# Differential attention beside a gated linear recurrence: no activation-table changes in the attention, the rotation on VectorE, both score maps as row tiles, and a three-part pool

## The chip, the cores and the metric

One Trainium2 chip, one core of it. The metric is the device time of one execution in microseconds (us). The kernel is written in Bass with its tile framework: the order on TensorE (PE) is the program's own, the other engines (VectorE, DVE; ScalarE, ACT; GpSimd, POOL; SyncE, SP) get their order from a scheduler that goes by priorities and dependencies. Line numbers L.. are those of the kernel before, unless the text says otherwise.

## The reference

One layer on 512 latent tokens (T) with 256 context tokens (C) ahead of them, width 1024. Three branches read the same modulated input: A, a bidirectional RG-LRU behind a convolution of width 4; B, differential attention with rotary positions, 8 heads of two maps with 64 dimensions each; C, a gated MLP. Cut to what the change touches:

```python
def diff_attn_core(q, k, v, lam):
    s = jnp.einsum('bqhmd,bkhmd->bhmqk', q.astype(f32), k.astype(f32)) * (DIFF_HEAD_DIM ** -0.5)
    p = jax.nn.softmax(s, axis=-1)
    w = p[:, :, 0] - lam * p[:, :, 1]
    return jnp.einsum('bhqk,bkhe->bqhe', w, v.astype(f32)).astype(v.dtype)
...
def diff_head_out(o, g, lam_init):
    of = o.astype(f32)
    of = of * lax.rsqrt(jnp.mean(jnp.square(of), axis=-1, keepdims=True) + RMS_EPS)
    of = of * g.astype(f32) * (1.0 - lam_init)
```

Each branch is multiplied by a SiLU gate (z * sigmoid(z)) of its own projection, projected, merged by sigmoid gates, projected again, and added to the input under a layer norm.

## The kernel before

Everything is float32 in and out. A product of two float32 matrices is made of three products of parts: each operand is split into a high part in the engine's rounded float32 (fp32r) and a low part, the rest, and TensorE adds high x high, high x low and low x high (`mm3`, L62 to L64; `proj_cm` for a whole projection of 24 products). Splitting is a cast on ScalarE and a subtraction (`split`, L54 and L55). Weights come by DMA on SP's queue in the order of a list of wants (`want`, L193 on), in pieces of 128 x 1024, and are split in `w_conv` (L121 the cast, L122 the subtraction, on POOL during the attention and on VectorE behind it).

The work goes in stages. A head (0 to 60 us) makes the modulated input. A prologue (60 to 98) projects q, k and v of the first heads. The attention (98 to 396) has 32 steps, one for each head h and block qt of 128 queries: `scores` (L705) makes both maps' scores, 768 keys each, into two of three PSUM buffers of 1024 columns; `softmax` takes the maximum (L715, VectorE) and the exponential (L720, ScalarE) of each and scales the first by 1/sum (L723); `combine` subtracts the second times lambda (L728 to L730, VectorE). Between the scores and the transposes of the step before (`transp`, L735, whose result is split in `wt_split`, L746 and L748) the hand-written plan puts units of projections for later heads: k, context k (kc), q, v, and the gate gb. Their evacuation is cut into chores that are handed out between units: `z_evac` (L512, ScalarE), `rope` (a shuffle L521, z times the cosine on POOL L522, the shuffled times the sine L524, the sum L525), then the split of q (`q_evac`, L542, L547) and k (`k_split`, L565, L570).

For the scores the high and low part of a map stand on the two halves of the 128 partitions of k: map 0 has its high part on partitions 0 to 63 and its low part on 64 to 127, map 1 the other way round. One product with K=128 then does two of the three at once, and needs q's parts on both halves, which a DMA on POOL's queue copies (L549). So a step has 8 products, four of 512 and four of 256 columns.

When a head's four blocks are done, `values` multiplies with v, squares on ScalarE (L755), evacuates (L756, VectorE), and `rms` sums the squares with a product with ones, takes Ln (L762) and Exp (L763) and multiplies on POOL (L764). The gate of the head takes a sigmoid (L670). Exponential, Ln and sigmoid are in different activation tables, and each change is an ACT_TABLE_LOAD on ScalarE.

The recurrence's stage (396 to 644) begins with the last transposes, the first block's projection xa0, head 7's values and its rms, the context's projection xac0; `conv_in` (L865, L867) evacuates both into `pad`, `conv` and `conv_split` make the input of the gate products ri. For each of 8 blocks follow the projections, the gates, the scans, the block's SiLU gate (`branch_a`, ga, which writes the block's result to DRAM in pa_d, L947), and the merge of branch B (`merge_gate` gt1, `merge_b` y1, which reads hsB, the split of all heads' outputs ob).

Behind it (from 644) pa_d is loaded back into pa on SP's queue (L1026) and split into hsA (L54, L55), and branch C begins: `proj_tokens` projects 16 pieces sv, each added on VectorE to the bias bvv (L1041 into vz), a load on SP's queue behind those of pa (L1031).

Of the kernel before, what the change touches and what calls it, by code (L numbers as in the profile page):

```python
# [22 lines left out]
H = 8  # L23
# [6 lines left out]
def block_kernel(ctx, tc, x, c, cctx_in, c_ctx, w_ada, b_ada, w_in, b_in, conv_w, conv_b,  # L30
# [193 lines left out]
    V.memset(tiny, 2.0 ** -100)  # L224
    sc16 = cp.tile([P, 16], F32, name="sc16")
# [18 lines left out]
    with tc.tile_pool(name="hd", bufs=1) as hd:  # L244
# [186 lines left out]
        S.preload_act_table_set("natural_log_exp_and_others")  # L431
# [72 lines left out]
    def z_evac(ps, b, name):  # L504
# [6 lines left out]
        z = at.tile([P, T], F32, tag="z", bufs=2, name="z" + name)  # L511
# [16 lines left out]
    def q_evac(h, ps):  # L528
# [5 lines left out]
        def hi():  # L534
            qds[h] = at.tile([P, 4, T], F32R, tag="qd", bufs=2, name="qd" + n)
            qd = qds[h]
            for m in range(2):
                a = slice(64 * m, 64 * m + 64)
                if h < 2:
                    S.mul(qd[a, 2 * m, :], z[a], 0.125)  # L540
                else:
                    V.tensor_scalar(qd[a, 2 * m, :], z[a], 0.125, None, op0=ALU.mult)  # L542

        def fin(m):
            qd = qds[h]
            a, b = slice(64 * m, 64 * m + 64), slice(64 - 64 * m, 128 - 64 * m)
            V.scalar_tensor_tensor(qd[a, 2 * m + 1, :], z[a], 0.125, f(qd[a, 2 * m, :]),  # L547
                                   op0=ALU.mult, op1=ALU.subtract)
            G.dma_start(qd[b, 2 * m:2 * m + 2, :], qd[a, 2 * m:2 * m + 2, :])  # L549
        chore(0.7, n, hi, 4 * h - 5)  # L550
        chore(0.6, n, lambda: fin(0))
        chore(0.6, n, lambda: fin(1))

    def k_split(n, h, z, sl):

        def hi():
            if h not in kds:
                kds[h] = at.tile([P, 2, TA], F32R, tag="kd", bufs=2, name=f"kd{h}")
            kd = kds[h]
            for m in range(2):  # L560
                a = slice(64 * m, 64 * m + 64)
                if n[1:] in "01":
                    S.copy(kd[a, m, sl], z[a])
                else:
                    V.tensor_copy(kd[a, m, sl], z[a])  # L565

        def lo(m):
            kd = kds[h]
            a, b = slice(64 * m, 64 * m + 64), slice(64 - 64 * m, 128 - 64 * m)
            V.tensor_tensor(kd[b, m, sl], z[a], f(kd[a, m, sl]), ALU.subtract)  # L570
        w = (sl.stop - sl.start) / 960
        chore(w + 0.15, n, hi, 4 * h - 5)
        chore(w + 0.07, n, lambda: lo(0))
        chore(w + 0.07, n, lambda: lo(1))
# [47 lines left out]
    def units(kind, i):  # L622
# [39 lines left out]
        def u():  # L662
# [7 lines left out]
            S.activation(sg, ps, AF.Sigmoid, bias=bcol(40 + i))  # L670
# [608 lines left out]
```

## Time and profile before

| | us |
|---|---|
| median of 3 runs | 1037.99 |
| lowest and highest run | 1035.18, 1039.12 |
| the profiled execution's own time | 1038.81 |
| its span in the trace | 1037.0 |
| TensorE (PE) busy | 974.0 (94%) |
| VectorE (DVE) busy | 663.6 (64%) |
| ScalarE (ACT) busy | 526.1 (51%) |
| GpSimd (POOL) busy | 155.7 (15%) |

The span is that of the profiled instructions; the execution's own time has 1.8 us around it. Busy time of TensorE counts a product to its modelled end, so the start times of products tell more than their lengths. A share of the whole span is an average over stages with different limits, so the rows below are those of single stages, waits and stretches. The granted clock (PEclk) is 1.00 at full speed.

### The profile page before, as it was taken

The numbers are of one execution on the slowest core, as the hardware profiler recorded it, in microseconds if no ns is written. First come the engines' busy times: TensorE is split into PE (matmuls) and PEld (weight loads), VectorE is DVE, ScalarE is ACT, GpSimd is POOL, SyncE is SP. The second block draws the span as 40 slices with busy tenths as digits, with TensorE's granted clock in tenths as the row PEclk, the third lists the DMA queues.
The fourth block names the chain that finished last, engine by engine and source line by source line (L and its number), as shares of the span: only waits on it lengthen the run. The fifth ranks groups of instructions, "written<-read, shape, count | busy, mean of one in ns | idle before, by whom it ended". The sixth has DMA issues, their size and how long they took to land.

```text
span 1037.0 us, 14225 instructions
## 1 busy us (share of the span) xinstructions
PE 974.0 (94%) x5719; PEld 844.0 (81%) x5719; DVE 663.6 (64%) x1024; ACT 526.1 (51%) x741; POOL 155.7 (15%) x117
## 2 busy tenths in 40 slices
PE   5997799989989998999999999599999999999996
PEld 4796688878878886888888888598889988888896
DVE  4479788788788663787777776348433356424567
ACT  3145856647647796897777794213231234332221
POOL 2143424333243252000000000000000000000002
PEclk8999999989989999999999999799999999999998
DMA  9933220130130132113333223534332232654312
GB/s 299 296 103 84 62 61 21 42 101 21 41 102 21 41 102 70 43 51 102 102 102 92 82 92 92 189 107 132 95 99 82 82 102 82 236 171 145 98 61 82
DMA packets 148184, 103.41 MB, mean 100 GB/s; under 512 B 3629, under 2 KB 143382, under 8 KB 148118
## 3 DMA queue, kind: packets, MB, share of 16 engines
q1 hardware_dynamic: 146054, 96.11, 30.4%
q0 software_dynamic: 1920, 6.29, 2.3%
q8 instruction: 45, 0.74, 0.3%
q14 instruction: 21, 0.17, 0.1%
q10 hardware_dynamic: 144, 0.10, 0.0%
HBM read 94.10 MB, written 4.19 MB: 95 GB/s over the span
## 4 chain that ended last, share of the span: by engine, by line
PE 66%; DVE 16%; ACT 10%; DMA 4%; issue 3%; SPq 1%; POOL 0%; POOLq 0%; ACTq 0%; DVEq 0%
PE y L62 4%; PE gt L62 4%; PE gt L64 4%; PE gt L63 4%; PE y L64 4%; PE y L63 4%; DVE mxn L715 2%; DVE e L730 2%; DVE kd L565 2%; PE out L62 1%; PE u L62 1%; PE u L64 1%; PE u L63 1%; PE out L64 1%; PE out L63 1%
## 5 line engine op out<-in xcount | busy, mean ns | idle before, releaser
L121 ACT CAST w<-raw 128x1024 fp32r<-128x1024 f32 x96 | 99.7, 1044 | 83.5 <-PE y L64 20.0
L122 DVE TENSOR_TENSOR w<-raw,w 128x1024 fp32r<-128x1024 f32 x71 | 86.4, 1222 | 66.9 <-ACT w L121 66.9
L62 PE MATMUL gt<-xhl,w 128*128 128x512 f32 x192 | 75.6, 394 | 1.3 <-ACT pad L865 1.3
L63 PE MATMUL gt<-xhl,w 128*128 128x512 f32 x192 | 74.8, 390 | 0.0
L64 PE MATMUL gt<-xhl,w 128*128 128x512 f32 x192 | 74.8, 390 | 0.0
L705 PE MATMUL s<-kd,qdq 128*128 128x512 f32 (+1 forms) x256 | 58.7, 368 | 15.6 <-ACT e L720 6.0
L122 POOL TENSOR_TENSOR w<-raw,w 128x1024 fp32r<-128x1024 f32 x25 | 61.0, 2445 | 67.4 <-ACT w L121 67.4
L705 PEld LDWEIGHTS s<-kd,qdq 128*128 128x128 f32 x256 | 44.5, 196 | 27.1 <-issue 12.7
L715 DVE TENSOR_REDUCE mxn<-s 128x1 f32<-128x768 f32 x64 | 58.3, 949 | 7.5 <-PE s L705 7.5
L720 ACT ACTIVATE e<-s,mxn 128x768 f32<-128x768 f32 x32 | 28.8, 900 | 50.9 <-DVE mxn L715 50.8
L1162 POOL PARTITION_BROADCAST grb<-grs x8 | 3.8, 581 | 322.4 <-DVE grs L1159 322.4
L62 PEld LDWEIGHTS gt<-xhl,w 128*128 128x128 f32 x192 | 36.1, 188 | 9.1 <-ACT pad L865 1.5
L64 PEld LDWEIGHTS gt<-xhl,w 128*128 128x128 f32 x192 | 36.0, 188 | 7.7
L63 PEld LDWEIGHTS gt<-xhl,w 128*128 128x128 f32 x192 | 36.1, 188 | 7.0
L947 POOL DMA_DIRECT2D pa_d<-ha x8 | 4.4, 551 | 227.4 <-DVE ha L946 227.4
L730 DVE SCALAR_TENSOR_TENSOR e<-s,sm,e 128x768 f32<-128x768 f32 x32 | 32.6, 1017 | 6.5 <-ACT e L723 5.7
L54 ACT CAST vh<-v 128x128 fp32r<-128x128 f32 x48 | 12.4, 264 | 42.7 <-PE v L64 19.5
L842 ACT ACT_TABLE_LOAD x25 | 32.1, 1283 | 0.5
L62 PE MATMUL xa<-xhl,w 128*128 128x512 f32 x64 | 26.3, 411 | 4.8 <-ACT pad L865 4.8
L748 DVE TENSOR_TENSOR wtl<-t,wth 128x768 fp32r<-128x768 f32 x32 | 30.3, 950 | 0.6 <-ACT wth L746 0.5
L723 ACT ACTIVATE e<-e,sm 128x768 f32<-128x768 f32 x32 | 29.9, 934 | 0.2 <-DVE sm L722 0.2
L842 ACT ACTIVATE rt<-ri,colB 128x770 f32<-128x770 f32 x32 | 27.7, 906 | 2.5 <-PE ri L64 1.8
(457 smaller groups left out, 3233.0 us busy)
## 6 DMA issues: line engine op xcount, KB each, us to landing
raw<-in_w_in_dram SPq DMA_DIRECT2D x96, 512.0 KB, 3.9
raw<-in_w_branch_dram SPq DMA_DIRECT2D x24, 512.0 KB, 4.0
ada<-in_w_ada_dram SPq DMA_DIRECT2D x6, 1024.0 KB, 9.6
qdq<-qdq POOLq DMA_DIRECT2D x16, 256.0 KB, 3.2
adg<-in_w_ada_dram SPq DMA_DIRECT2D x8, 512.0 KB, 6.6
raw<-in_w_out_dram SPq DMA_DIRECT2D x8, 512.0 KB, 3.4
xtok<-in_x_dram SPq DMA_DIRECT2D x4, 512.0 KB, 5.7
ada<-in_w_ada_dram SPq DMA_DIRECT2D x4, 512.0 KB, 5.9
```

The lines of the kernel that those rows point to most:

```text
L62: PE.matmul(ps, ah, bh, start=(first and i == 0), stop=False)
L63: PE.matmul(ps, ah, bl, start=False, stop=False)
L64: PE.matmul(ps, al, bh, start=False, stop=(last and i == n - 1))
L121: S.copy(h, raws[j])
L122: state["lo"].tensor_tensor(l, raws[j], f(h), ALU.subtract)
L705: PE.matmul(sp[:, sl], qds[h][:, 2 * m + j, qs], kds[h][:, m, sl], start=(j == 0), stop=(j == 1))
L715: V.tensor_reduce(mxn[:, m:m + 1], sps[m][:, 0:TA], mybir.AxisListType.X, ALU.max, negate=True)
L720: S.activation(e, sps[m][:, 0:TA], AF.Exp, bias=mxn[:, m:m + 1], accum_out=sm[:, m:m + 1])
L723: S.mul(es[i][0], es[i][0], sm[:, 0:1])
L730: V.scalar_tensor_tensor(e0, e1, sm[:, 1:2], e0, op0=ALU.mult, op1=ALU.add)
L748: V.tensor_tensor(wts[h][1][:, :, qs], src, f(wts[h][0][:, :, qs]), ALU.subtract)
L842: order[0] = S.activation(out, in_, fn, **kw)
```

## The change

It has five parts.

- **No table changes in the attention.** The gate's sigmoid(x) becomes 0.5 * tanh(0.5 x) + 0.5 in two ScalarE passes, tanh being in the exponential's table. `rms` keeps only the mean square: the product with 32 columns of ones writes 32 rows, which are copied into msb, four heads one above the other. Ln and Exp are taken once for all heads behind head 7. The 8 rows of 1/rms go to DRAM by 8 DMAs on POOL's queue, come back on SP's queue to all partitions (rsb, in five loads on two shared buffers), and `hs_b` multiplies them into ob on VectorE and splits ob into hsB.
- **Rotation on VectorE alone.** The product with the cosine moves from POOL to VectorE.
- **Both maps side by side.** q and k keep map 0 on partitions 0 to 63 and map 1 on 64 to 127, with the high and the low part in two planes; high parts are made on ScalarE in one instruction for both maps, low parts on VectorE in one. The copying DMAs go. Each of the three products has K=64 and a tile position of its own, row 0 or row 64, and the two maps alternate: 12 products a step.
- **Softmax and evacuation.** The second map's exponential goes to SBUF in place of PSUM. The evacuation of o moves from VectorE to ScalarE.
- **The pool in three parts.** mp (msb, sq), a1 (the rotation's tiles, z, zc) and at (the rest). a1 is released at step 28 and its space taken by l1, into which the recurrence's first weights are loaded there. In TensorE's order xac0 comes ahead of head 7's values, xa1, xac1 and a gate gt1 ahead of the first gates ri. Behind the recurrence bvv is loaded ahead of pa, and the last piece of pa by POOL's queue.

```diff
@@ rope @@
-            G.tensor_tensor(z, z, ropc, ALU.mult)
-        chore(0.6, name, c0)
+            V.tensor_tensor(z, z, ropc, ALU.mult)
+        chore(1.3, name, c0)
@@ q_evac @@
+            qds[h] = at.tile([P, 2, T], F32R, tag="qd", bufs=2, name="qd" + n)
+            S.mul(qds[h][:, 0, :], z, 0.125)
+
+        def lo():
             qd = qds[h]
...
-            G.dma_start(qd[b, 2 * m:2 * m + 2, :], qd[a, 2 * m:2 * m + 2, :])
+            V.scalar_tensor_tensor(qd[:, 1, :], z, 0.125, f(qd[:, 0, :]),
                                    op0=ALU.mult, op1=ALU.subtract)
@@ k_split @@
+            S.copy(kds[h][:, 0, sl], z)
...
+            V.tensor_tensor(kd[:, 1, sl], z, f(kd[:, 0, sl]), ALU.subtract)
@@ the gate gb, in units @@
-            S.activation(sg, ps, AF.Sigmoid, bias=bcol(40 + i))
+            S.activation(sg, ps, AF.Tanh, bias=hb[:, i:i + 1], scale=0.5)
+            S.activation(sg, sg, AF.Identity, bias=halfc, scale=0.5)
...
-            S.preload_act_table_set("natural_log_exp_and_others")
@@ scores @@
+        sps = [big_t(f"s{i}_{m}") for m in range(2)]
+        for sl in (slice(0, 512), slice(512, TA)):
+            for j, (jq, jk) in enumerate(((0, 0), (0, 1), (1, 0))):
+                for m in range(2):
+                    a = slice(64 * m, 64 * m + 64)
+                    PE.matmul(sps[m][:, sl], qds[h][a, jq, qs], kds[h][a, jk, sl],
+                              start=(j == 0), stop=(j == 2), tile_position=(64 * m, 0))
@@ softmax @@
-            e = sps[1][:, 0:TA]
-            if m == 0:
-                e = at.tile([P, TA], F32, tag="e0", bufs=2, name=f"e0_{i}")
+            e = at.tile([P, TA], F32, tag=f"e{m}", bufs=2 - m, name=f"e{m}_{i}")
@@ values @@
-        V.tensor_scalar(ob[:, h, :], ps, vbias[:, h:h + 1], gcol, op0=ALU.add, op1=ALU.mult)
+        S.activation(ob[:, h, :], ps, AF.Identity, bias=vbg[:, h:h + 1], scale=gcol)
@@ rms @@
-        PE.matmul(pm, ones, sq, start=True, stop=True)
-        S.activation(sq, pm, AF.Ln, bias=epst)
-        S.activation(sq, sq, AF.Exp, scale=-0.5)
-        G.tensor_tensor(ob[:, h, :], ob[:, h, :], sq, ALU.mult)
+        r = slice(32 * (h % 4), 32 * (h % 4) + 32)
+        PE.matmul(pm[r, 0:T], ones[:, 0:32], sq, start=True, stop=True,
+                  tile_position=(0, 32 * (h % 4)))
+        order[0] = S.copy(msb[r, h // 4, :], pm[r, 0:T])
@@ in the loop over steps @@
+        if i == 28:
+            a1.release()
+            l1 = tc.alloc_tile_pool(name="l1", bufs=1, side="right", reuse_waits="tile")
+            lru_dma(0)
+            pad = pad_alloc()
@@ behind the loop @@
+    with tc.high_priority():
+        conv_in(0, ps, True)
+    ps = acc_t("xac0")
+    proj_cm(ps[:, 0:TC], W, C, 0, TC)
+    with tc.high_priority():
+        conv_in(0, ps[:, 0:TC], False)
+        conv(0)
+        lru_hi(0)
     sqs.append((7, values(7, big_t)))
...
+    act(msb, msb, AF.Ln, bias=epst)
+    act(msb, msb, AF.Exp, scale=-0.5)
+    for h in range(H):
+        r = 32 * (h % 4)
+        G.dma_start(rs_d[h:h + 1, :], msb[r:r + 1, h // 4, :])
...
+    def hs_b(n, hs_):
+
+        rsb = mp.tile([P, len(hs_), T], F32, tag=("sq", "msb")[len(hs_) - 1], name=f"rsb{n}")
+        for j, h in enumerate(hs_):
+            nc.sync.dma_start(rsb[:, j, :], rs_d[h].partition_broadcast(P))
+        for j, h in enumerate(hs_):
+            V.tensor_tensor(ob[:, h, :], ob[:, h, :], rsb[:, j, :], ALU.mult)
+            split(hs[:, 0, h, :], hs[:, 1, h, :], ob[:, h, :])
@@ in the recurrence's loop @@
+        if i == 0:
+            merge_gate(0)
...
+        if i == 0:
+            for n, hs_ in enumerate(((0, 1), (2,), (3, 4), (5,), (6, 7))):
+                hs_b(n, hs_)
@@ behind it @@
-    for g in range(8):
-        nc.sync.dma_start(pa[:, g, :], pa_d[g])
+    for g in range(7):
+        nc.sync.dma_start(pa[:, g, :], pa_d[g])
+    G.dma_start(pa[:, 7, :], pa_d[7])
```

How the built programs' orders differ at three places. A name's numbers tell its buffers apart; rows read line, operation, out<-in, shape. First TensorE, the third step's scores behind the transposes (t) of the step before. Before:

```order
L735 MATMUL t_1178<-ident,e_2_1075 128x128 x6
L705 MATMUL s_0_1192<-kd_737,qdq_778 128x512 x2
L705 MATMUL s_0_1192<-kd_737,qdq_778 128x256 x2
L705 MATMUL s_1_1197<-kd_737,qdq_778 128x512 x2
L705 MATMUL s_1_1197<-kd_737,qdq_778 128x256 x2
L62 MATMUL q_1214<-xhl,w_995 128x512
```

and with the change:

```order
L727 MATMUL t_1193<-ident,e_2_1085 128x128 x6
L700 MATMUL s_0_1204<-kd_776,qdq_780 128x512
L700 MATMUL s_1_1205<-kd_776,qdq_780 128x512
L700 MATMUL s_0_1204<-kd_776,qdq_780 128x512
L700 MATMUL s_1_1205<-kd_776,qdq_780 128x512
L700 MATMUL s_0_1204<-kd_776,qdq_780 128x512
L700 MATMUL s_1_1205<-kd_776,qdq_780 128x512
L700 MATMUL s_0_1204<-kd_776,qdq_780 128x256
L700 MATMUL s_1_1205<-kd_776,qdq_780 128x256
```

Six pairs (the last four products of 256 columns are left out) take the place of eight products, and neither map is done before the other.

Next ScalarE where head 6's rms and a gate fall, in steps 26 and 27: sq is the squares, ms their sum, lw the recurrence's weights, sgb the gate, e the exponentials. Before:

```order
L762 ACT_TABLE_LOAD
L762 ACTIVATE sq_3196<-ms_3241,epst 128x512
L763 ACT_TABLE_LOAD
L763 ACTIVATE sq_3196<-sq_3196 128x512
L720 ACTIVATE e_26_3259,sm_3256<-s_0_3246,mxn_3257 128x768
L720 ACTIVATE s_1_3251,sm_3256<-s_1_3251,mxn_3257 128x768
L723 ACTIVATE e_26_3259<-e_26_3259,sm_3256 128x768
L670 ACT_TABLE_LOAD
L670 ACTIVATE sgb_3298<-gb_3268,colC 128x512
L746 CAST wth_3206<-t_3303 128x6x128
L720 ACT_TABLE_LOAD
```

and with the change:

```order
L748 ACTIVATE ob<-o_3247,vbg,gcol 128x512
L738 CAST wth_3276<-t_3269 128x6x128
L784 CAST lwh_3850<-lw_3536 128x512
L54 CAST vh_2819<-v_4_3280 128x128
L757 COPY msb<-ms_3309 32x512
L54 CAST vh_2886<-v_4_3280 128x128
L712 ACTIVATE e_26_3329,sm_3326<-s_0_3312,mxn_3327 128x768
L712 ACTIVATE e_26_3332,sm_3326<-s_1_3313,mxn_3327 128x768
L715 ACTIVATE e_26_3329<-e_26_3329,sm_3326 128x768
L664 ACTIVATE sgb_3369<-gb_3339,hb 128x512
```

The four table loads are gone, a copy of 32 rows stands where Ln and Exp stood, and the cast of the recurrence's first weights has moved in ahead of the exponentials of step 26.

Last VectorE at the end of the recurrence, with the queues and engines that a row waits for (DMAHW are transfers of SP's queue, DMASW those of POOL's). Before:

```order
L946 TENSOR_TENSOR ha_5450<-ha_5450,sga_5581 128x512 [waits DVE_49]
L55 TENSOR_TENSOR hsA<-pa,hsA 128x512 [waits DMAHW7_49,Activation_49]
L55 TENSOR_TENSOR hsA<-pa,hsA 128x512 [waits DMAHW0_49,Activation_49]
L55 TENSOR_TENSOR hsA<-pa,hsA 128x512 [waits DMAHW1_49,Activation_49]
L55 TENSOR_TENSOR hsA<-pa,hsA 128x512 [waits DMAHW2_49,Activation_49]
L55 TENSOR_TENSOR hsA<-pa,hsA 128x512 [waits DMAHW3_49,Activation_49]
L55 TENSOR_TENSOR hsA<-pa,hsA 128x512 [waits DMAHW4_49,Activation_49]
L55 TENSOR_TENSOR hsA<-pa,hsA 128x512 [waits DMAHW5_49,Activation_49]
L55 TENSOR_TENSOR hsA<-pa,hsA 128x512 [waits DMAHW6_49,Activation_49]
L1041 TENSOR_TENSOR vz<-sv_0_5606,bvv 128x256 [waits DMAHW7_49,PE_49]
```

and with the change:

```order
L970 TENSOR_TENSOR ha_5610<-ha_5610,sga_5709 128x512 [waits DVE_49]
L55 TENSOR_TENSOR hsA<-pa,hsA 128x512 [waits DMASW0_49,Activation_49]
L1069 TENSOR_TENSOR vz<-sv_0_5736,bvv 128x256 [waits DMAHW7_49,PE_49]
L1069 TENSOR_TENSOR vz<-sv_1_5768,bvv 128x256 [waits PE_49]
L55 TENSOR_TENSOR hsA<-pa,hsA 128x512 [waits DMAHW0_49,Activation_49]
L55 TENSOR_TENSOR hsA<-pa,hsA 128x512 [waits DMAHW1_49,Activation_49]
```

Of the eight subtractions one is left ahead of the first sum vz, and that one waits for a transfer of POOL's queue: it is the last piece of pa.

## Rows read from the trace of the kernel before

**Rows 1.** The page's part 4, the chain that ended last, by engine.
```profile
PE 66%; DVE 16%; ACT 10%; DMA 4%; issue 3%; SPq 1%; POOL 0%; POOLq 0%; ACTq 0%; DVEq 0%
```

**Rows 2.** Busy time in the attention; columns: window, length, each engine's busy us, PEclk, DMA.
```profile
98.00:396.00 298.00, 279.94 (x1592) 241.90 (x1591) 231.00 (x402) 201.18 (x324) 105.91 (x63) 0.97 0.20 55
```

**Rows 3.** TensorE's waits: prologue, attention, recurrence; us in total, times, longest.
```profile
PE v L62 <- DVE vl L55: 4.7, 1, 4.7
...
PE s L705 <- ACT e L720: 6.0, 3, 2.2
PE s L705 <- issue: 5.4, 1, 5.4
PE s L705 <- DVE e L730: 4.3, 4, 1.9
PE v L62 <- DVE vl L55: 2.1, 4, 0.6
...
PE sv L62 <- DVE vz L1041: 11.7, 1, 11.7
PE xa L62 <- ACT pad L865: 4.8, 1, 4.8
PE gt L62 <- ACT pad L865: 1.3, 1, 1.3
```

**Rows 4.** Half-clock stretches: sum of the first five, then two with clock 0.51, 0.50.
```profile
sum 23.80, PE 20.11 PEld 18.14 DVE 21.22 ACT 17.54 POOL 10.78; mean PE 4.02 PEld 3.63 DVE 4.24 ACT 3.51 POOL 2.16
...
412.90:419.80 6.90, 5.59 (x13) 4.43 (x14) 5.24 (x6) 6.27 (x13) 2.75 (x2) 0.51 0.32 94
651.90:665.50 13.60, 4.38 (x20) 4.39 (x21) 5.95 (x10) 4.83 (x8) 0.00 (x0) 0.50 0.73 261
```

**Rows 5.** ScalarE's groups in the attention: line, operation, count, busy us, mean ns.
```profile
L762 ACT ACT_TABLE_LOAD x7 | 9.0, 1283 | 0.1
...
L762 ACT ACTIVATE sq<-ms,epst 128x512 f32<-128x512 f32 x7 | 4.8, 688 | 0.1
```

**Rows 6.** VectorE's groups in the attention.
```profile
L565 DVE CAST kd<-zc 64x256 fp32r<-64x256 f32 x12 | 13.7, 1145 | 0.2
...
L524 DVE TENSOR_TENSOR t1k<-t1k,rops 128x512 f32<-128x512 f32 x6 | 4.1, 689 | 0.2
```

**Rows 7.** Timeline, POOL and VectorE, from 123 us: start, us, instruction.
```profile
123.43 5.36 POOL L122 TENSOR_TENSOR w10l<-raw,w10h 128x1024 fp32r<-128x1024 f32 x2 [1.45 <-issue]
...
123.93 2.67 DVE L525 TENSOR_TENSOR zk<-zk,t1k 128x512 f32<-128x512 f32 x1
```

**Rows 8.** The tile pa_d: from issue to landing of its eight transfers.
```profile
DMA to landing us min/median/max: 2.3/2.5/6.3
```

**Rows 9.** Timeline of TensorE around the SGU's gr, into and out of it.
```profile
950.06 0.39 PE L63 MATMUL y<-hsC,w 128*128 128x512 f32 x1
950.29 0.39 PE L64 MATMUL y<-hsC,w 128*128 128x512 f32 x1
950.61 0.65 PE L1156 MATMUL gr<-adg,w32o 128*32 128x128 f32 x16
...
952.49 0.50 PE L62 MATMUL y<-hsC,w 128*128 128x512 f32 x1
952.83 0.40 PE L63 MATMUL y<-hsC,w 128*128 128x512 f32 x1
```

**Rows 10.** Timeline of TensorE, two products of 256 columns in a row.
```profile
406.12 0.28 PE L64 MATMUL xac<-chl,w 128*128 128x256 f32 x1
406.24 0.28 PE L62 MATMUL xac<-chl,w 128*128 128x256 f32 x1
```

**Rows 11.** Timeline of ScalarE at the start of the recurrence.
```profile
409.66 1.28 ACT L762 ACT_TABLE_LOAD   x1
...
413.49 0.67 ACT L865 ACTIVATE pad<-xa,colC 128x512 f32<-128x512 f32 x1
```

**Rows 12.** Timeline behind the recurrence: POOL's write of pa_d, VectorE's first vz.
```profile
647.72 0.54 POOL L947 DMA_DIRECT2D pa_d<-ha x1 [13.23 <-DVE ha L946]
...
660.64 0.76 DVE L1041 TENSOR_TENSOR vz<-sv,bvv 128x256 f32<-128x256 f32 x2 [1.26 <-DMA bvv<-in_b_in_dram]
```

More of the change, by code (lines that the diff above doesn't have):

```diff
@@ L558, in hi, with lo @@
                 kds[h] = at.tile([P, 2, TA], F32R, tag="kd", bufs=2, name=f"kd{h}")
+            S.copy(kds[h][:, 0, sl], z)
+        def lo():
             kd = kds[h]
[L560 to L570, printed above, removed]
+            V.tensor_tensor(kd[:, 1, sl], z, f(kd[:, 0, sl]), ALU.subtract)
         w = (sl.stop - sl.start) / 960
-        chore(w + 0.15, n, hi, 4 * h - 5)
-        chore(w + 0.07, n, lambda: lo(0))
-        chore(w + 0.07, n, lambda: lo(1))
+        chore(0.1, n, hi, 4 * h - 5)
+        chore(w + 0.15, n, lo)
     def k_evac(h, ps):
@@ L688, in block_kernel @@
         drain(2.0)
-    es, sms, wts = {}, {}, {}
+    es, sms, order = {}, {}, [None]
     def hp(on):
@@ L778, in finish, with lru_dma, lru_hi, lru_w @@
             rms(*sqs.pop(0))
+    lraw, lws, xcs, xhl2, RIA, has, sgs = {}, {}, {}, {}, {}, {}, {}
+    NJ = T + 2 + TC
+    def lru_dma(g):
+        wl = l1.tile([P, 4, P], F32, tag="lw", bufs=1, name=f"lw{g}")
+        for j, w in enumerate((lru_wa, lru_wx)):
+            nc.sync.dma_start(wl[:, j:4:2, :], w[0, :, g].rearrange("d p q -> p d q"))
+        lraw[g] = wl
+    def lru_hi(g):
+        lws[g] = [l1.tile([P, 4, P], F32R, tag="lwh", bufs=1, name=f"lwh{g}"), None]
+        S.copy(lws[g][0], lraw[g])
+    def lru_w(g):
+        if g not in lws:
+            lru_hi(g)
+        lws[g][1] = lr.tile([P, 4, P], F32R, tag="lwl", bufs=1, name=f"lwl{g}")
+        V.tensor_tensor(lws[g][1], lraw[g], f(lws[g][0]), ALU.subtract)
+        if g < 7:
+            lru_dma(g + 1)
+    def pad_alloc():
+        pad = l1.tile([P, 773], F32, name="pad")
+        for a, b in ((0, 2), (514, 516), (772, 773)):
+            V.memset(pad[:, a:b], 0.0)
+        return pad
+    def conv_in(g, ps, lat):
+        if lat:
+            S.activation(pad[:, 2:514], ps, AF.Identity, bias=bcol(g))
+        else:
+            S.activation(pad[:, 516:772], ps, AF.Identity, bias=bcol(g))
+    def conv(g):
+        xc = l1.tile([P, NJ], F32, tag="xc", bufs=2, name=f"xc{g}")
+        V.tensor_scalar(xc, pad[:, 0:NJ], colB[:, g:g + 1], colB[:, 32 + g:33 + g],
+                        op0=ALU.mult, op1=ALU.add)
+        for jj in range(1, 4):
+            V.scalar_tensor_tensor(xc, pad[:, jj:jj + NJ], colB[:, 8 * jj + g:8 * jj + g + 1], xc,
+                                   op0=ALU.mult, op1=ALU.add)
+        xcs[g] = xc
     sqs = []
```

135 lines of the change are left out of this document (45 added, 90 removed).

## The prediction

> **What bounds the kernel now.** I read the chain of waits first: TensorE is two thirds of what ended last, VectorE and ScalarE most of the rest [rows 1]. So I went to the stages. In the attention, 98 to 396 us, TensorE is busy for 279.94 of 298.00 us, VectorE for 231.00 and ScalarE for 201.18 [rows 2]: TensorE bounds the stage, and the other two matter only where it waits for them. The third view is TensorE's waits by what it waited for [rows 3]: up to the attention's end 4.7 + 6.0 + 5.4 + 4.3 + 2.1 = 22.5 us, at the start of the recurrence 4.8 + 1.3, at its end one of 11.7. The fourth is the granted clock. After such a wait TensorE runs for some microseconds at its lower level, 1.2 instead of 2.4 GHz, and half of its busy time there is lost. Five such stretches up to the attention's end hold 20.11 us of busy TensorE, so 10.1 us are lost; the one at the start of the recurrence costs 5.59/2 = 2.8, the one behind its end 4.38/2 = 2.2 [rows 4]. That is 22.5 + 10.1 + 6.1 + 2.8 + 11.7 + 2.2 = 55.4 us that the change can reach; the rest of the span is TensorE at work.
>
> The sum is made against the profiled execution, 1038.81 us; the median of the runs is 0.8 lower. About 0.5%, 5 us, is what a measurement of this kernel can tell from no change.
>
> **The attention's waits and clock.** The change takes four loads off the engines that TensorE waits for.
>
> Table loads: by the instruction order 31 fewer are left in the attention, 1.28 us each [rows 5]. In this stage the trace has 26 (four groups, of which one stands in the rows): 33.4 us of ScalarE. Ln and Exp of seven heads go too, 14 x 0.69 = 9.7 us. Added are seven halvings of the gate, seven copies of a mean square and seven evacuations of o, 21 passes of 512 columns like that Ln, 14.5 us, and the high halves of q, k and kc of six heads, 6 x (0.69 + 0.69 + 0.35) = 10.4. ScalarE falls by 33.4 + 9.7 - 14.5 - 10.4 = 18 us.
>
> Halves and copies: VectorE loses the casts of 64 rows, among them 12 of kc at 1145 ns, and writes each low half once for 128 rows, not twice for 64. It gains 12 products of the rotation, 0.69 us each if nothing holds them [rows 6], 8 us in all. POOL loses those, the products with 1/rms and the 16 copying DMAs.
>
> POOL's hold on VectorE: while POOL splits two weight pieces, for 5.36 us, an add of 512 columns takes VectorE 2.67 us [rows 7], against 0.69 for the same form free [rows 6]; it ends as POOL's piece does. This stays, since POOL still splits the weights. The rotation's products can be held in the same way, and now the combining of the maps too, which reads two operands from SBUF where it read one from PSUM. Twelve held products are 12 x 2 = 24 us more of VectorE, less than it has idle (298 - 231 = 67).
>
> Score buffers: the second map's buffer now comes free after its exponential, not after the combining; that answers to the 4.3 us of waits for L730.
>
> Wait by wait I leave 1 of the prologue's 4.7 (the rotation is off POOL there), half of the 5.4, which lies behind the pair of weight pieces of rows 7 and is the least cured, 1.5 of the 6.0 for the exponential, 0.5 of the 4.3, and 1 of the 2.1: 6.7 of 22.5 stay, 15.8 go. Of the clock I leave one stretch of five, 1.6 us: 8.5 go. Sum **-24.3**. The ends are all, -32, and almost nothing, -5; I stand nearer the first, since removed work or a freed buffer answers to four of the five waits.
>
> The early load of the recurrence's first weights puts a ScalarE cast into step 26 that waits for its DMA, with that step's exponentials behind it. Five instructions stand between the last split of q and that cast, so I cost it at nothing; uncovered it is a landing, like the 2.5 us of pa_d [rows 8].
>
> **The scores.** A step has four products of 512 and four of 256 columns at K=128; a start follows the last by 0.23 us with 512 columns [rows 9] and by 0.12 with 256 [rows 10]: 4 x (0.23 + 0.12) = 1.40 us. Afterwards it has six pairs of K=64. If both of a pair run at once and all else is free: 3 x 0.35 = 1.05, or -0.35 a step, -11 in 32. The nearest row of tiles side by side is the SGU's gr, 64 products from 950.61 to 952.49, 29 ns each, four at a time. It also shows what a change of shape costs: into it 0.32 in place of 0.23, out of it 0.34, so 0.20 us a step [rows 9]. Each product loads its own 128 stationary columns. The trace has no such pair, so its two loads lie between hidden (a 256 pair takes 0.12) and one behind the other (0.24). I take 0.16, nearer to gr's, whose loads run beside each other: 3 x (0.23 + 0.16) + 0.20 = 1.37. Sum **-1** (ends: -11; +7 with 3 x (0.23 + 0.24) + 0.20 = 1.61).
>
> Rows 9 thus price a change of shape at about 0.1 us. The Trainium skill, page "TensorEngine Tiling (Array Packing)", section "Key Properties", says that a change of the tiling mode drains TensorE, and so speaks against 64 new changes; it gives no price, and by that rule this term could only rise. The Trainium skill, page "TensorE: Matmul & The Clock Gate", section "Measured speedup vs the span model", has four row tiles at 3.07 times one; with two at nearly twice, an estimate from that page, and the changes of rows 9 the term would be -11 + 6 = -5 and the sum 4 lower, as in rival 1. No row here shows row tiles.
>
> **The start of the recurrence.** Before, 4.8 + 1.3 us of waits and 2.8 of clock: the evacuation of xa0 stands on ScalarE behind Ln, Exp and two table loads [rows 11]. Now xa0 and xac0 are evacuated ahead of head 7's values, and xa1, xac1 and gt0 stand ready for TensorE, so nearly all of the 8.9 goes. What comes: 1/rms goes through DRAM. From head 7's mean square on: copy, two loads, Ln and Exp of twice the columns, 0.7 + 2.6 + 2.8 = 6 us; the write, 2.5 at the median landing [rows 8]; three rounds of a load and two products, since two buffers are shared, 3 x (2.5 + 1.4) = 12; about 20 us. Before y0 needs the last head TensorE has xa1, xac1, gt0, four gates, xa2, xac2 and two gates: 24 x (3 x 0.23 + 2 x 0.12) + 6 x 3 x 0.35 = 28 us. With the longest landing, 6.3 us [rows 8], it is 6 + 6.3 + 3 x 7.7 = 35, and 7 show. The products and splits on VectorE also stand ahead of the next block's xcl. I take 5 us of new waits: **-4** (ends -8 and +5).
>
> **The end of the recurrence.** Before, eight loads of pa stand on SP's queue ahead of the bias bvv; the first sum vz waits for that bias until 660.64 [rows 12], and TensorE for vz, 11.7 us [rows 3]. The change issues bvv first. But in the built order vz stands on VectorE behind the low half of hsA[7], whose source is the last pa: written to DRAM from 647.72 [rows 12], read back by POOL's queue, cast on ScalarE, subtracted. Write and read take 2.5 to 6.3 us each [rows 8], cast and subtraction 1.4. With the middle of each 647.7 + 4.4 + 4.4 + 1.4 = 657.9, with POOL's issue about 658.5: **-2** (ends -6 and +3).
>
> **Sum.** -24.3 - 1 - 4 - 2 = -31.3: 1038.8 - 31.3 = 1007.5 for a profiled execution, **1007** for the median.
>
> **The rivals.**
> 1. *All of it works*: the waits all but go (-28), the pairs run as in gr (-5), and vz does not wait for pa (-11.7 - 2.2), as where hsA[7] falls into a time that TensorE fills. 1038 - 28 - 5 - 4 - 14 = 987 (978 to 995). For it: removed work; against: the order of vz. Chance 0.17.
> 2. *The waits move*: VectorE, held by POOL at its new products and at the combining, is late for the next scores as before; half of the 24.3 comes back, and the DRAM trip costs 6 more. 1038 - 12 - 1 + 2 - 2 = 1025 (1018 to 1035). For it: rows 7; against: 67 us of idle VectorE. Chance 0.12.
> 3. *The paired products run one behind the other* (the other side). Then a step has 12 starts in a row: 6 x 0.35 + 0.20 = 2.30 us, +0.90, in 32 steps +29; the softmax begins later by as much each time, and a third of the regained waits, 8 us, returns. 1007 + 1 + 29 + 8 = 1045 (1035 to 1056). It decides from a step of 1.40 + (31 - 8)/32 = 2.1 us. For it: no row shows K=64; against: gr's tiles do run side by side. Chance 0.08.
> 4. *The change does not do what it says*: table loads stay in the attention. The instruction order shows none there, so it gets no chance.
>
> **How the numbers follow.** The forecast, with its terms' ends half taken, spans 996 to 1019; it has 0.63. The range, 984 to 1030, takes in most of rivals 1 and 2. Faster: 0.63 + 0.17 + 0.08 of rival 2 = 0.88; within 0.5% (1032.8 to 1043.2): the other 0.04 of it and 0.02 of rival 3 = 0.06; slower: the 0.06 left of rival 3.
>
> **What would show it.** Right: in the attention no table loads, ScalarE near 183 us, TensorE's waits under 8 us, one half-clock stretch at most; a pair's second product starting some ns after its first, a step near 1.37 us; no long wait at y0; the wait for vz still there, 8 to 11 us, now released through hsA. Wrong: a pair's starts 0.2 us apart (rival 3); VectorE operations of 2 to 5 us beside POOL's pieces with scores waiting (rival 2); no wait at vz (rival 1).

## The result, and the profile after

The changed kernel is slower by 0.7%: 1045.2 us median (1044.63 to 1047.91) beside 1038.55 for the kernel before, a ratio of 1.0073 with a 95% interval of 1.0054 to 1.0091. The forecast was 1007, range 984 to 1030. The profiled execution has a span of 1042.9 us, 5.9 more than before.

TensorE's waits after, three views by stretch (80 to 393.6 is the attention, to 454.9 the first block of the recurrence, then the rest to the first sums of branch C), against [rows 3]:

```profile
PE o L63 <- DVE wtl L740: 11.5, 6, 2.2
PE s L700 <- ACT e L712: 5.2, 3, 4.0
PE v L62 <- DVE vl L55: 3.9, 3, 1.3
...
PE y L62 <- ACT pad L802: 4.5, 1, 4.5
PE ri L63 <- DVE xcl L906: 2.5, 1, 2.5
...
PE sv L62 <- DVE vz L1069: 15.3, 1, 15.3
```

The prologue's wait of 4.7 us for vl is gone, and of the scores' three waits (15.7 us) 5.2 are left; 4.0 of these stand ahead of the second scores, at 97.09, still in the prologue's 60 to 98 us. In their place stand a wait in six of the heads' values, new ones at y and ri, and a longer one at vz. By equal pieces of work, from TensorE's first product of one unit to the first of another, the 5.9 us come together like this:

| piece of TensorE's work | before | after | difference |
|---|---|---|---|
| v of the prologue | 62.30 to 86.04 | 62.47 to 79.98 | -6.2 |
| from there to xa0 (the attention) | to 395.77 | to 393.64 | +3.9 |
| xa0 to the end of the first y and of the second block's gates | to 455.84 | to 454.94 | +1.2 |
| to the first sv | to 643.54 | to 646.34 | +3.7 |
| to the end of the span | to 1037.0 | to 1042.9 | +3.1 |

(Another 0.2 lie ahead of the first row.) The attention by kinds of units, times summed from first start to next unit's first start, steps 1 to 31: scores 63.8 before, 44.8 after; transposes 25.0 and 26.6; mean squares 3.3 and 6.8; values 30.3 and 47.1; projections 179.1 and 179.9. Scores, transposes and mean squares together fell from 92.1 to 78.2 us, so most of the waits for scores went, as forecast. The values took the gain.

**The values.** VectorE and TensorE after, timeline from 170 us, head 1:

```profile
170.03 0.76 DVE L533 STREAM_SHUFFLE t1q<-zq 128x512 f32<-128x512 f32 x1
170.82 2.78 DVE L534 TENSOR_TENSOR zq<-zq,ropc 128x512 f32<-128x512 f32 x1
173.52 0.68 DVE L536 TENSOR_TENSOR t1q<-t1q,rops 128x512 f32<-128x512 f32 x1
174.12 0.94 DVE L740 TENSOR_TENSOR wtl<-t,wth 128x768 fp32r<-128x768 f32 x1
...
170.46 0.81 ACT L738 CAST wth<-t 128x768 fp32r<-128x768 f32 x1
170.65 2.41 POOL L122 TENSOR_TENSOR w<-raw,w 128x1024 fp32r<-128x1024 f32 x1 [6.30 <-ACT w L121]
...
172.86 0.39 PE L62 MATMUL o<-wth,vh 128*128 128x512 f32 x1
175.12 0.50 PE L63 MATMUL o<-wtl,vh 128*128 128x512 f32 x1 [1.87 <-DVE wtl L740]
```

POOL begins a weight piece at 170.65; the rotation's product, new on VectorE, begins at 170.82 and takes 2.78 us, until 0.5 us after the piece has ended. wth is ready at 171.27, but its low half stands behind the rotation on VectorE and starts at 174.12; TensorE has begun the values at 172.86 and waits. The product's group shows that it is so for every q and for no k (VectorE's groups after, 98 to 390 us):

```profile
L534 DVE TENSOR_TENSOR zq<-zq,ropc 128x512 f32<-128x512 f32 x6 | 16.1, 2685 | 0.2
...
L534 DVE TENSOR_TENSOR zk<-zk,ropc 128x512 f32<-128x512 f32 x6 | 4.2, 692 | 0.2
```

In the kernel before, at the same place, the rotation's sum stood behind wtl (VectorE's timeline before):

```profile
177.01 1.81 DVE L715 TENSOR_REDUCE mxn<-s 128x1 f32<-128x768 f32 x2
178.74 0.95 DVE L748 TENSOR_TENSOR wtl<-t,wth 128x768 fp32r<-128x768 f32 x1
...
179.67 1.48 DVE L525 TENSOR_TENSOR zq<-zq,t1q 128x512 f32<-128x512 f32 x1
```

**The shape.** One step late in the attention, TensorE's timeline before and then after:

```profile
387.02 0.82 PE L735 MATMUL t<-ident,e 128*128 128x128 f32 x6
387.59 1.65 PE L705 MATMUL s<-kd,qdq 128*128 128x512 f32 x8
389.07 0.40 PE L62 MATMUL gb<-xhl,w 128*128 128x512 f32 x1
389.30 0.40 PE L63 MATMUL gb<-xhl,w 128*128 128x512 f32 x1
```

```profile
384.49 0.82 PE L727 MATMUL t<-ident,e 128*128 128x128 f32 x6
385.24 1.32 PE L700 MATMUL s<-kd,qdq 64*128 64x512 f32 x12
386.49 0.50 PE L62 MATMUL gb<-xhl,w 128*128 128x512 f32 x1
386.83 0.40 PE L63 MATMUL gb<-xhl,w 128*128 128x512 f32 x1
```

The twelve products take 1.25 us (385.24 to 386.49), the eight took 1.48 (387.59 to 389.07). In the trace their starts lie 3 to 4 ns apart by pairs; 512-column pairs follow each other by 0.33, 0.23, 0.23 us, 256-column pairs by 0.12. So the pairs do run side by side, their loads too. But the transposes ahead take 0.75 in place of 0.57, and the first product behind 0.34 in place of 0.23. From the first transpose to the second product behind the scores it is 2.28 us before (387.02 to 389.30) and 2.34 after (384.49 to 386.83): what the pairs save is spent on the way in and out, and little more.

A mean square (ms) ahead of scores, before and then after:

```profile
379.19 1.12 PE L761 MATMUL ms<-sq,ones 128*128 128x512 f32 x2
379.75 1.96 PE L705 MATMUL s<-kd,qdq 128*128 128x512 f32 x8
381.54 0.40 PE L62 MATMUL gb<-xhl,w 128*128 128x512 f32 x1
381.78 0.40 PE L63 MATMUL gb<-xhl,w 128*128 128x512 f32 x1
...
376.65 1.05 PE L755 MATMUL ms<-sq,ones 128*32 128x512 f32 x2
377.63 1.31 PE L700 MATMUL s<-kd,qdq 64*128 64x512 f32 x12
378.87 0.50 PE L62 MATMUL gb<-xhl,w 128*128 128x512 f32 x1
379.21 0.40 PE L63 MATMUL gb<-xhl,w 128*128 128x512 f32 x1
```

From the mean square to the scores it is 0.98 us, against 0.56 before. But before the same time was lost one row later, where the eight products took 1.79: to the second product of gb it is 2.59 before and 2.56 after. Steps with the same neighbours, at full clock and with nothing waiting, differ by 0.0 to 0.08 us, and by 0.17 where v stands ahead of the mean square. Over the 31 steps that adds up to some 2 us, an estimate from these starts.

**Behind the attention.** Three rows of the new DRAM trip, then SP, POOL, ScalarE and VectorE at the end of the recurrence (timeline after), against [rows 12]:

```profile
422.12 11.00 SPq L897 DMA_DIRECT2D rsb<-rs_d  x6
434.35 0.47 SPq L897 DMA_DIRECT2D rsb<-rs_d  x1
442.33 0.68 DVE L899 TENSOR_TENSOR ob<-ob,rsb 128x512 f32<-128x512 f32 x1
...
650.90 0.50 SPq L1050 DMA_DIRECT2D bvv<-in_b_in_dram  x1
651.50 5.96 SPq L1057 DMA_DIRECT2D pa<-pa_d  x7
651.31 0.54 POOL L971 DMA_DIRECT2D pa_d<-ha  x1 [2.99 <-DVE ha L970]
660.04 0.55 POOL L1058 DMA_DIRECT2D pa<-pa_d  x1 [8.18 <-DMA pa_d<-ha]
...
666.65 0.69 DVE L55 TENSOR_TENSOR hsA<-pa,hsA 128x512 fp32r<-128x512 f32 x1 [15.64 <-ACT hsA L54]
667.26 0.75 DVE L1069 TENSOR_TENSOR vz<-sv,bvv 128x256 f32<-128x256 f32 x2
```

The last of the rsb loads is issued at 434.35, behind six that waited for their two buffers, and the last product with it is done at 443.0. At the end, the write of the last pa is issued at 651.31, beside the seven loads and bvv; it is landed at 660.0, 8.2 us after it began to wait, and the read at 665.9.

### The profile page after: what moved, and what is told of

It is laid out like the page before. It is cut to its first block, busy times and chain, and to the rows that moved or that the text cites. A ratio compares the mean times of both kernels' runs of the same rounds, so it can differ in the third digit from the quotient of the medians.

```text
span 1042.9 us, 14354 instructions
## 1 busy us (share of the span) xinstructions
PE 974.6 (93%) x5847; PEld 831.2 (80%) x5847; DVE 644.0 (62%) x983; ACT 500.6 (48%) x734; POOL 111.8 (11%) x86
## 4 chain that ended last, share of the span: by engine, by line
PE 68%; DVE 15%; ACT 9%; DMA 4%; issue 2%; SPq 1%; POOL 0%; POOLq 0%; DVEq 0%; ACTq 0%
PE y L62 4%; PE y L63 4%; PE y L64 4%; PE gt L62 4%; PE gt L63 4%; PE gt L64 4%; ACT e L712 3%; DVE mxn L709 2%; DVE zq L534 2%; PE out L62 1%; PE u L62 1%; PE u L64 1%; PE u L63 1%; PE out L64 1%; PE out L63 1%
## 5 line engine op out<-in xcount | busy, mean ns | idle before, releaser
L712 ACT ACTIVATE e<-s,mxn 128x768 f32<-128x768 f32 x64 | 57.5, 901 | 74.8 <-DVE mxn L709 74.8
L700 PEld LDWEIGHTS s<-kd,qdq 64*128 64x128 f32 x384 | 32.4, 185 | 20.7 <-issue 9.6
L700 PE MATMUL s<-kd,qdq 64*128 64x256 f32 (+1 forms) x384 | 43.9, 353 | 5.2 <-ACT e L712 5.2
L722 DVE SCALAR_TENSOR_TENSOR e<-e,sm,e 128x768 f32<-128x768 f32 x32 | 32.6, 1018 | 12.0 <-ACT e L715 11.4
L63 PE MATMUL o<-wtl,vh 128*128 128x512 f32 x48 | 21.5, 448 | 11.5 <-DVE wtl L740 11.5
L62 PE MATMUL y<-hsB,w 128*128 128x512 f32 x64 | 26.0, 407 | 4.5 <-ACT pad L802 4.5
```

What stands on the lines that cost most here:

```text
L62: PE.matmul(ps, ah, bh, start=(first and i == 0), stop=False)
L63: PE.matmul(ps, ah, bl, start=False, stop=False)
L700: PE.matmul(sps[m][:, sl], qds[h][a, jq, qs], kds[h][a, jk, sl], start=(j == 0), stop=(j == 2), tile_position=(64 * m, 0))
L712: S.activation(e, sps[m][:, 0:TA], AF.Exp, bias=mxn[:, m:m + 1], accum_out=sm[:, m:m + 1])
L722: V.scalar_tensor_tensor(e0, e1, sm[:, 1:2], e0, op0=ALU.mult, op1=ALU.add)
```

## The experiments

Each kernel was timed beside the kernel before on the same chip; that one's median lay between 1038.3 and 1039.4 us each time. "Both mends" are those of e5 and e2 together.

**e1.** The rotation's product back on POOL.

```diff
-            V.tensor_tensor(z, z, ropc, ALU.mult)
-        chore(1.3, name, c0)
+            G.tensor_tensor(z, z, ropc, ALU.mult)
+        chore(0.6, name, c0)
```

> The changed kernel with one part undone: the rotation's product with the cosine goes back from VectorE to POOL. Theory A (that product, held on VectorE for 2.78 us while POOL splits a weight, stands ahead of the low half wtl that TensorE's values wait for): the values' waits for wtl (11.5 us, six of some 1.9) go to under 2, a first product pair of values takes 4.2 instead of 6.3 us per head, and with the clock the time falls by 12 to 19 us, to 1026 to 1033. Theory B (VectorE and ScalarE are simply later with the transposes' halves, whatever stands ahead): the waits stay above 8 us and the time within 4 us of 1045. Theory C (the paired products alone make the loss): no change either, within 4 us.

Measured: 1056.62 us, 1.0181 of before (1.0156 to 1.0206), 11 slower than the change, which none of the three had. The values' waits grew (TensorE's waits, then VectorE's timeline):

```profile
PE o L63 <- DVE wtl L740: 19.9, 6, 3.5
```

```profile
177.47 2.83 DVE L537 TENSOR_TENSOR zq<-zq,t1q 128x512 f32<-128x512 f32 x1 [1.19 <-POOL zq L534]
180.22 0.94 DVE L740 TENSOR_TENSOR wtl<-t,wth 128x768 fp32r<-128x768 f32 x1
```

The rotation's sum now waits for POOL's product and is then held by the weight piece behind it, still ahead of wtl. Theory A had the wrong instruction: not the product on VectorE is at fault, but anything of the rotation that POOL delays and that stands ahead of wtl.

**e5.** The attention's low halves of weights on VectorE.

```diff
-    state["lo"] = G
+    state["lo"] = V
```

> The changed kernel, but the low halves of the attention's weights are made on VectorE (1.2 us each) and not on POOL; the rotation's product stays on VectorE. Theory A (POOL's pieces hold VectorE): no VectorE operation of 512 columns of the rotation takes more than 0.8 us, the values' waits for wtl fall below 4 us although VectorE gets some 25 x 1.2 = 30 us more work; time 1030 to 1040. Theory B (VectorE has too much ahead of wtl): 30 us more work make the waits longer, above 12 us, and the time 1048 or more. Theory C: within 4 us of 1045.

Measured: 1023.45 us, 0.9855 (0.9836 to 0.9874), 21.8 below the change. The wait of the values for wtl is gone, and the product is at its free price, with 18 weight pieces of 1.26 us added in the same stretch (VectorE's groups, 98 to 380 us, then its timeline at head 1):

```profile
L122 DVE TENSOR_TENSOR w<-raw,w 128x1024 fp32r<-128x1024 f32 x18 | 22.7, 1262 | 7.5 <-ACT w L121 7.3
...
L534 DVE TENSOR_TENSOR zq<-zq,ropc 128x512 f32<-128x512 f32 x6 | 4.1, 691 | 0.2
```

```profile
159.15 0.69 DVE L534 TENSOR_TENSOR zq<-zq,ropc 128x512 f32<-128x512 f32 x1
159.76 0.69 DVE L536 TENSOR_TENSOR t1q<-t1q,rops 128x512 f32<-128x512 f32 x1
160.36 0.95 DVE L740 TENSOR_TENSOR wtl<-t,wth 128x768 fp32r<-128x768 f32 x1
```

It is POOL's hold, and not VectorE's load. In five of the six heads the rotation still stands ahead of wtl, as here, and the values do not wait: the place alone, without the hold, costs them nothing. The gain is above what theory A allowed, since the wait of 4.0 us for the exponential and the four half-clock stretches of the attention went too.

**e7.** POOL keeps the weights; the rotation is ordered behind wtl.

```diff
-            V.stream_shuffle(t[0], z, shmask)
-            V.tensor_tensor(z, z, ropc, ALU.mult)
+            with tc.issue_after(wtl_last[0].ins) if wtl_last[0] else ExitStack():
+                V.stream_shuffle(t[0], z, shmask)
+                V.tensor_tensor(z, z, ropc, ALU.mult)
...
+            wtl_last[0] = V.tensor_tensor(wts[h][1][:, :, qs], src, f(wts[h][0][:, :, qs]),
+                                          ALU.subtract)
```

> The changed kernel with the rotation's shuffle and product ordered behind the last low half wtl on VectorE; POOL still splits the weights. Theory A2 (it is the place ahead of wtl that costs, the hold only sets how much): the values' waits for wtl, 11.5 us, go under 2 though single products still take over 2 us; the time falls by 12 to 18 us, to 1027 to 1033. The rival (the hold comes back elsewhere: maxima, the next scores): other waits of TensorE in the attention grow by 6 us or more and the time falls by less than 6, to 1039 or more.

Measured: 1035.6 us, 0.9957 (0.9945 to 0.9969), 9.6 below the change. No wait for wtl is left among TensorE's waits; those of v for vl rose from 3.9 to 7.2, and the 5.2 for the exponential stayed (5.4). But the products are not held in their new place (0.69 us in the mean of six), so e7 takes away the place and the hold at once, and its condition of products still over 2 us did not come about. Other holds stay: the low half of kc (kd from zc) takes 2.08 us each in six, as after the change (2.09), and the values do not wait for it. With e5 this says that the values paid for a held instruction ahead of wtl, and for neither half of that alone. The other 12 us that e5 gains lie in the scores (47.7 us in e7 and 40.6 in e5, from the first scores to xa0) and the transposes with the waits behind them (32.3 and 28.5); the wait of 4.0 for the exponential, which e7 has and e5 has not, is among them.

**e9.** Both mends, the rotation's product on POOL (the edit of e1).

> The changed kernel with both mends (POOL splits no weights in the attention), but the rotation's product on POOL. It alone tells what the rotation on VectorE is worth when POOL holds nothing long: a product on POOL took 1.80 us against 0.69 and holds VectorE's sum behind it. If the place ahead of wtl matters, the values' waits come back by some 1 us each, 6 us in all: 1021 to 1026. If not: 1014 to 1019.

Measured: 1026.8 us, 0.9881 (0.9862 to 0.9901), 8.9 above both mends alone and just above the expected 1021 to 1026. The values wait again (2.8 us in six; 33.8 us in all for 29.4) and v of the prologue takes 1.2 us more: the rotation on VectorE alone is a gain of 9 us where POOL splits no weights. POOL still holds here, with the product itself, and what it holds is a weight piece ahead of wtl (VectorE and POOL, timeline):

```profile
127.27 2.31 DVE L122 TENSOR_TENSOR w<-raw,w 128x1024 fp32r<-128x1024 f32 x1
129.51 0.94 DVE L740 TENSOR_TENSOR wtl<-t,wth 128x768 fp32r<-128x768 f32 x1
...
126.70 1.79 POOL L534 TENSOR_TENSOR zq<-zq,ropc 128x512 f32<-128x512 f32 x1 [11.73 <-DVE t1q L533]
```

The piece takes 2.31 us, where e5's took 1.26 in the mean.

**p1.** The kernel before, with the pairs alone.

```diff
-            for sl in (slice(0, 512), slice(512, TA)):
-                for j in range(2):
-                    PE.matmul(sp[:, sl], qds[h][:, 2 * m + j, qs], kds[h][:, m, sl],
+            for j, (jq, jk) in enumerate(((0, 0), (0, 1), (1, 0))):
+                for m in range(2):
+                    PE.matmul(sps[m][:, sl], qds[h][a, jq, qs], kds[h][a, jk, sl],
+                              start=(j == 0), stop=(j == 2), tile_position=(64 * m, 0))
...
```

> The kernel before with one part of the change alone: both maps side by side (K=64 pairs, 12 products a step, split q and k in planes of 128 rows, no copying DMAs). If the changed kernel's trace reads right, a step's scores and the changes of shape around them cost 0.15 us more than eight products (the transposes before them 0.75 for 0.57, the scores 1.25 for 1.38, the unit behind 0.1 more), +5 us in 32 steps; VectorE has some 25 us less to do, which gives back up to 8 of the attention's waits: 1034 to 1044. Theory C (the pairs make the loss): 1044 to 1050.

Measured: 1047.22 us, 1.0086 (1.0065 to 1.0107), 8.9 slower. The pairs alone lose what the whole change loses, and the time lies in theory C's range, but not by the pairs' own price: a wait of the values for wtl came with them (10.1 us; the values take 41.0 us for 30.3), though nothing of the rotation was edited. The rotation's sum moved ahead of wtl here too, held by a weight piece (2.86 us in the mean of six, 1.47 before); why the scheduler moved it was not tried.

**b5, p5.** The kernel before with the low halves on VectorE (the edit of e5), and the same with the pairs.

> The kernel before with the low halves of the attention's weights made on VectorE and not on POOL. If POOL's hold is what VectorE's lateness comes from in the kernel before too, the wait of 5.4 us at 124 and most of the waits for the combining and the values' low halves go, some 10 of the 17.8 us and half of the clock's loss: 1024 to 1031. If VectorE, with 231 of 298 us busy, has no room for 25 x 1.2 = 30 us more: 1038 or more.

> The kernel before with the weights' low halves on VectorE and both maps side by side. Without POOL's hold, the difference to the same kernel without the pairs is the pairs' own price. Read from the changed kernel's trace it is +0.15 us a step, +5 us in all (twelve weight loads of 0.117 us bound the step at what eight products took, and two changes of shape come on top); range +2 to +8. The rival, that pairs pay once nothing else waits: -3 or less.

Measured: 1028.2 (0.9898; 0.9878 to 0.9918) and 1036.78 us (0.9973; 0.996 to 0.9986). The one-line edit gives the kernel before 11 us, and the pairs cost 8.6 on top of it, just outside the expected +2 to +8. That is not the pairs' own price: the values take 46.7 us in p5 and 29.5 in b5. In p5 a weight piece, held by POOL's rotation product (2.31 us at 136.95), and two maxima stand on VectorE ahead of wtl, and the values wait 11.2 us for it; in b5 it is v that waits, 10.2 us on VectorE. The +0.15 us a step of the two expectations was wrong as well. It set the scores against 1.38 us, which eight products take behind a projection; behind transposes they take 1.48. Nor do twelve loads stand in a row: they start in pairs, 3 to 4 ns apart. No run isolates the pairs; the 2 us from the starts stay an estimate.

**e2, e8.** vz ahead of hsA, alone and with e5's edit.

```diff
-        split(hsA[:, 0, g, :], hsA[:, 1, g, :], pa[:, g, :])
+        S.copy(hsA[:, 0, g, :], pa[:, g, :])
+        with tc.issue_after(vzs[6].ins):
+            V.tensor_tensor(hsA[:, 1, g, :], pa[:, g, :], f(hsA[:, 0, g, :]), ALU.subtract)
...
```

> The changed kernel with VectorE's subtractions for hsA put behind the seventh sum vz. The wait of 15.3 us is then not for pa but for the bias bvv, issued at 650.9: it lands 6 to 7 us later, so the wait falls to 4 to 7 us and the time by 8 to 13 us with the clock, to 1032 to 1037. The rival, that another late input (weights cast behind hsA on ScalarE) takes its place: a new wait of 5 us or more for a weight of sv, and the time within 4 us of 1045.

> The changed kernel with both mends: weights' low halves on VectorE, and the sums vz ahead of hsA. If the two are independent their gains add, 21.8 + 5.9 us: 1016 to 1019. If one hides part of the other: 1020 to 1023.

Measured: 1039.33 us (1.0008; 0.9998 to 1.0018) and 1017.88 (0.9793; 0.9778 to 0.9808). The wait at vz fell from 15.3 to 7.3 us; the time only by 5.9, less than the 8 to 13 expected. The two mends add up: 21.8 + 5.9 = 27.7, measured 27.3.

**e6.** Both mends, and 1/rms spread by TensorE in place of the DRAM trip.

```diff
-            nc.sync.dma_start(rsb[:, j, :], rs_d[h].partition_broadcast(P))
+            PE.matmul(ps[:, j * T:(j + 1) * T], ones[r, :], msb[r, h // 4, :], start=True,
+                      stop=True, tile_position=(32 * (h % 4), 0))
...
```

> The changed kernel with both mends, and 1/rms brought to all partitions by eight TensorE products with a block of ones (K=32) and not through DRAM. Theory (the DRAM trip's three rounds cause the waits at y0, 5.1 us, and at the next block's gates, 3.0): both go, eight products and four shape changes cost 4 to 5 us of TensorE, the clock's loss behind the wait goes: 1012 to 1017 against 1017.9. The rival (VectorE's and ScalarE's products, casts and subtractions for eight heads are what y0 waits for, wherever 1/rms comes from): the wait stays, and the time rises by the products to 1020 to 1023.

Measured: 1016.43 us, 0.9775 (0.975 to 0.98), 1.5 below e8, and the intervals overlap. The eight products take 2.1 us, y0's wait is 3.2 for 5.1, the gates' 1.8 for 3.0. Part of the waits goes and the products pay for it: inconclusive on the time, and some 5 us of wait stay wherever 1/rms comes from.

**e10.** Both mends, the gate's sigmoid back in its own table.

```diff
-            S.activation(sg, ps, AF.Tanh, bias=hb[:, i:i + 1], scale=0.5)
-            S.activation(sg, sg, AF.Identity, bias=halfc, scale=0.5)
+            S.activation(sg, ps, AF.Sigmoid, bias=bcol(40 + i))
```

> The changed kernel with both mends, but the gate's sigmoid back in its own table: 8 sigmoids in place of 16 passes, and some 14 to 16 table loads of 1.28 us in the attention again, 20 us of ScalarE less 5. If ScalarE's table loads stood in TensorE's way, as the prediction had it for the exponential's waits: 4 us or more slower, 1022 or more. If ScalarE has room for them: within 3 us of 1017.9.

Measured: 1020.0 us, 0.9821 (0.9798 to 0.9844), 2.1 above e8, and the intervals overlap. Fifteen table loads came back (8 at the gate, 7 at the exponential), 19 us of ScalarE, at a price that is not clear of the noise. It is a test in a kernel where POOL splits no weights; the loads of Ln and Exp, the other half, were not put back.

**e11.** e6, with bvv loaded during the recurrence into the space of msb and hsA's casts behind sv's weights.

```diff
+    bvt = mp.tile([P, 2, T], F32, tag="msb", name="bvv")
+    nc.sync.dma_start(bvv, b_in[0, 7 * D:8 * D].partition_broadcast(P))
     branch_a(7)
...
```

> The kernel with both mends and 1/rms by TensorE, and the bias bvv loaded during the recurrence into the space of the mean squares; hsA's casts stand behind the weight casts of the second sv column. The wait of 8.4 us before the second and third sv goes, and with it a half-clock stretch (3.4 us): 1003 to 1009 against 1016.4. The rival, that a weight of sv or pa is late next: a wait of 4 us or more in that stage, 1010 to 1016.

Measured: 1004.21 us, 0.9662 (0.9646 to 0.9678). No wait at sv is left among TensorE's waits; this one beats both kernels, by 34.9 and 41.0 us.

The change without its pairs was not tried.

## Why the prediction was wrong

**The waits for scores** (part of the -24.3) mostly went, as forecast: 22.5 us of waits up to the attention's end, of which 6.7 were to stay; of the same rows 5.2 + 3.9 = 9.1 stayed. ScalarE has no table loads there. In e10 half of the loads, put back where POOL splits no weights, cost 2.1 us, not clear of the noise; whether the loads had a part in the kernel before was not tried. What freed the scores, the loads, the split planes, the evacuations or the score buffer, no run separates.

**The step that failed first** is "twelve held products are 24 us more of VectorE, less than it has idle". The size was no larger than that: of the twelve the six of q were held, 2.0 us each too long, 12 us. The combining began beside none of POOL's pieces and took 1.02 us in the mean, as before. But idle time elsewhere pays nothing for an instruction that stands ahead of one TensorE waits for. I asked how much VectorE had left, and not what is queued behind the held product: wtl, and behind that the values. They took 16.8 us more (30.3 to 47.1): 11.5 of waits, and 5.1 in three half-clock stretches behind such waits (135.5, 176.4, 254.9; TensorE is busy for all of their 3.4 us, at a granted clock of 0.50). Rival 2 had the mechanism, with the wait at the next scores in place of the values, and at 1025. The order of VectorE was there to be read before; wtl stands in it behind the rotation.

**The change of shape** at 0.20 us a step, from gr [rows 9], was a term that was mis-sized, by some 3 us. The side-by-side part was better than forecast: the pairs run at 0.23 and 0.12, the ideal. The changes cost 0.18 ahead, 0.10 at the first pair and some 0.2 behind, 0.48 a step; the eight products, on the other side, took 1.48 behind transposes where I had 1.40. In all it is about +2 against a forecast of -1. I priced from one place with 64 products between two changes, and left out that the first product on each side slows as well. Rival 3's time came out, 1045, by another road: no product ran behind its partner. By the rule on "Key Properties" of the page "TensorEngine Tiling (Array Packing)" of the Trainium skill, that a change of mode drains TensorE, the term could only rise; the trace agrees, the transposes ahead of the pairs take 0.75 us for 0.57.

**The start of the recurrence**, forecast -4, came out at +1.2. The waits of 8.9 went; 7.0 + 0.8 of new ones came, and a half-clock stretch of 10.3 us with 5.80 busy (439.2 to 449.5), 2.9 lost. The three rounds took 25 us from the first load to the last product (417.7 to 443.0), where I summed 12: the loads landed in 3.7 to 4.2 us and not in 2.5, and the time that each waits for products and a free buffer on VectorE was not in my sum. By e6 the trip through DRAM is only part of the waits: some 5 us stay without it. The next blocks then cost 3.7 more, which I had at nothing: ri, gt and ga wait 0.6 + 1.1 + 0.8 us near the end, where before one wait of 0.5 stood; what cost the rest is not shown.

**The end of the recurrence**, forecast -2, came out at +3.1. The chain was right (hsA[7] ahead of vz), its sizes were not: the write took 8.2 us and the read 5.9, where I took 4.4 for each; both run beside the loads of the other pieces. The write was also issued 3.6 us later than before, 2.8 of which the row above holds already. For the read a row was there: the loads of pa in the kernel before landed in 4.1 to 6.3 us, 6.0 in the median. e2 shows the chain at work: with vz put ahead of hsA 5.9 us go.

**The prologue**'s wait for vl went, as forecast; the 4.0 us for the exponential in the same stretch were not foreseen. **The sum** missed by 38 us; the values are some 17 of it, the shapes 3, the other waits that stayed 2, the recurrence's first and later blocks 9, its end 5.

## What to carry to other kernels

When an instruction gets slower or is moved to another engine, look in the built order at what stands behind it on that engine and who waits for that; the idle share of the engine answers another question. Here one line, the weights' low halves moved off POOL, was worth 22 us after the change and 11 before it. Before pairing small products, price a whole visit, from the unit ahead to the second product behind, in both shapes: here it was 2.28 us before and 2.34 after, and a piece of it alone (0.98 for 0.56 ahead of the scores) misleads.

## What the runs showed that was not expected

Products of K=64 on the two row halves start 3 to 4 ns apart and hide each other's loads: a pair of 256 columns every 0.12 us, as one product before. Behind a mean square, a product of ones over 512 columns, some 0.4 us are lost whichever shape follows: 0.98 us for 0.56 ahead of the pairs, or 1.79 us for eight products that take 1.38 behind a projection. A VectorE product with two SBUF operands takes 0.69 us, or 2.69 in the mean of six where a POOL piece of 2.4 us had begun just before; of the same form, six of k were never held, so it is the meeting and not the form that costs. wtl, which reads the transposes from PSUM, is not held: in e7 it takes 0.96 us at 171.61, inside a POOL piece from 170.96 to 173.37, for 0.95 elsewhere. A POOL product of 1.80 us holds too: a weight piece takes VectorE 2.31 us beside it. A write of 256 KB to DRAM landed in 2.3 us at the least and 2.7 in the median, and in 8.3 beside eight loads at the end of the recurrence.
